# One hybrid encoder layer on one core: attention's unit issued as one group, the convolution's norm held back, and two weights prepared a head ahead

## The chip, the cores and the metric

The kernel runs on one core of one Trainium2 chip. The metric is the device time of one execution in microseconds (us), lower is better. The program is one launch, traced once in Python and ordered by a planner that works with simulated times.

## The reference

The layer works on 2048 tokens of 1024 channels (float32), with a memory of 256 rows for cross attention.

```python
y = rmsnorm(h, norm_mix_g) @ w_in                      # 3*512 for q, k, v; 2*512 for the convolution
att = dilated_sliding_attention(rotary(q), rotary(k), v)   # 8 heads of 64; windows (128,1), (512,4), (2048,16)
conv = silu(layernorm(depthwise_conv31(a * sigmoid(g)) + conv_b))
h = h + concat([att, conv]) @ w_out
xq, xk, xv = rmsnorm(h) @ w_xq, rmsnorm(mem) @ w_xk, rmsnorm(mem) @ w_xv     # 4 heads of 256
h = h + (softmax(xq @ xk.T / 16) @ xv) @ w_xo
h = h + square(relu(rmsnorm(h) @ w_up)) @ w_down       # 4096 hidden
return rmsnorm(h, norm_final_g)
```

The sliding attention computes three dilation patterns, each with its own softmax, and mixes them by their log-denominators. Every depthwise output sums 31 taps.

## The kernel before, in words

**Precision.** Almost every product is made of three: each operand is split into a high and a low float32r part, and `mm3` (lines 200 to 202) issues high x high and the two mixed products. A weight comes as `raw` by DMA, ScalarE copies its high part, VectorE subtracts to get the low part (lines 190 and 191; 385 and 386 in the memory stage).

**Stages.** First comes a memory stage (`memory`, together with `xprep`, which normalises and transposes x). It projects mem with w_xk (`pxk`), multiplies the result with the transposed w_xq, head by head, into `ascr` (`pa`), projects mem with w_xv (`pxv`) and multiplies that with w_xo into `bscr` (`pb`). So the passes need neither w_xq nor w_xo. Then follow the linear layers of w_in (`lin`, `lin_v` with its evictions `vst`, line 576), with the convolution's taps of token block 0 beside them (`cacc`, line 217, on VectorE). Then comes the far stage: attention of token block 0 (512 tokens) with all patterns, the far one among them, beside the rest of `lin` as filler and beside `conv_ln(0)`, the convolution's layer norm of block 0. Four passes follow, one for each block of 512 tokens: `post(p)` does w_out (`o`), the cross attention's scores (`xs`) and output (`x`), and the MLP (`up`, `dn`). Beside passes 0 to 2 run attention of the next block (`att(p + 1)`, 0.95 of its steps to a step of the pass) and the convolution of the next block (`conv`, 0.6 of a step). The last pass has no such side work.

**Attention's unit.** A unit is half of a head's block for one pattern. It has three pieces: scores `s` (four products of 256 columns, line 1003) with VectorE's mask and minimum (`sm`, line 774) and ScalarE's exponential (line 775); the turn, four transposes `pt` (line 781), copied into f16 `ph` by ScalarE and `pl` by VectorE (lines 784, 785); and `opt`, twelve f16 products with v (lines 789 to 791). A block has 32 near units (8 heads, 2 patterns, 2 halves). In `att`, a round steps the newest unit's scores, yields, then steps the turn of the unit before and `opt` of the one before that, and yields again. `combine` mixes the patterns (transposes `catT`, line 948).

**What sets the order.** Code is traced in the order that the generators are stepped (`weave`). Each engine executes its own queue in order. The planner fills the queues from simulated times: of the instructions that are ready on an engine it takes the one traced first, so a later one can go ahead while the earlier ones are not ready. `tc.issue_after(x)` forbids that for one engine: every instruction traced inside the block stays behind x on x's engine. `last` holds the last marked instruction of each engine, `after` opens such a block for some engines, and `pinned(gen, ...)` does so at each step of a generator. Marked on VectorE (`last["dve"]`) are, among others, the evictions in `lin`, `lin_v` and `post`, and attention's mask step.

**The norm.** `conv_ln(n)` loads the four channel groups (`lc`, from `cscr`), sums them (`lsum`, lines 240 to 242), takes column sums on TensorE (line 237), subtracts the mean (line 250), squares, divides, and applies silu. For block 0 it is pinned on TensorE alone; in the passes it is not pinned.

**The memory stage's tiles.** Its weights rotate through four sets of raw, high and low tiles (`wtiles`: two named with m..., two that borrow x's tiles). For w_xq a set is loaded, transposed on TensorE (`xqt`, line 416), copied (line 418) and subtracted (line 419).

Of the kernel before, what the change touches and what calls it, by code (L numbers as in the profile page):

```python
# [16 lines left out]
ALU = mybir.AluOpType  # L17
# [4 lines left out]
P = 128  # L22
S = 2048
D = 1024
# [6 lines left out]
XH = 4  # L31
# [12 lines left out]
def f(ap):  # L44
    return ap.bitcast(F32)


def hybrid_layer(ctx, tc, A, out):
# [7 lines left out]
    def dma(o, i, q=None):  # L56
        (q or nc.sync).dma_start(o, i)
# [10 lines left out]
    def ps(kind, name, shape=(P, 512), dtype=F32):  # L68

        if isinstance(banks[kind], str):  # L70
            kind = banks[kind]
        n = turn.get(kind, 0)
        turn[kind] = n + 1
        return psp.tile(list(shape), dtype, tag=f"bank{banks[kind][n % len(banks[kind])]}", name=name)
# [119 lines left out]
    def wcols(w, c0, n=P, rows=None):  # L194
        v = w.rearrange("(k p) m -> p k m", p=P)
        return v[:, :, c0:c0 + n] if rows is None else v[:, rows[0]:rows[1], c0:c0 + n]
# [151 lines left out]
    def memory(sp):  # L348
        nat = [load_nat(sp, A["mem"][0, P * j:P * (j + 1), :], f"mn{j}") for j in range(2)]
        mh, ml = ([xpool(q, i, 3, f"m{q}{i}", (P, 4, NMEM)) for i in range(2)] for q in "hl")  # L350
        for k2 in range(KC // 2):
            pt = ps("b", f"mt{k2}")
            for e in range(2):
                for j in range(2):
                    PE.transpose(pt[:, e * 256 + j * P:e * 256 + (j + 1) * P],
                                 nat_cols(nat[j], 2 * k2 + e), ident)
            for e in range(2):
                k = 2 * k2 + e
                hv, lv = mh[k // 4][:, k % 4, :], ml[k // 4][:, k % 4, :]
                src = pt[:, e * 256:(e + 1) * 256]  # L360
                ACT.activation(hv, src, AF.Copy, scale=gain("mem", k))
                DVE.scalar_tensor_tensor(lv, src, gain("mem", k), f(hv), op0=ALU.mult, op1=ALU.subtract)
        r = rstd_nat(sp, nat, "m")
        rb = ps("c", "rbm")
        bcast_rows(rb, r, 2)
        DVE.tensor_copy(rmem[:, 0:2], r[:, 0:2])
        rbm = sp.tile([P, 2, NMEM], F32, tag="rbm", name="rbm")
        for q in range(2):
            ACT.activation(rbm[:, q], rb[:, 0:NMEM], AF.Copy, scale=-1.0 / 16.0)
        yield  # L370
        cnt = [0]

        def wtiles(name, shape=(P, 8, P)):
            i = cnt[0] % 4
            cnt[0] += 1
            if i < 2:
                return [wp.tile(list(shape), dt, tag=t, name=f"m{t}_{name}", bufs=2)
                        for t, dt in (("raw", F32), ("whi", F32R), ("wlo", F32R))]
            return [xpool(q, j, 2, f"m{q}{j}_{name}", shape, dt)
                    for q, j, dt in (("h", i - 2, F32), ("h", i, F32R), ("l", i, F32R))]  # L380

        def split(src, name, shape=(P, 8, P)):
            raw, hi, lo = wtiles(name, shape)
            dma(raw, src)
            ACT.copy(hi, raw)
            DVE.tensor_tensor(lo, raw, f(hi), op=ALU.subtract)
            return hi, lo

        def proj(w, name, th, tl):

            for j in range(KC):
                wh, wl = split(wcols(w, j * P), f"{name}{j}")
                pt = ps("mm", f"p{name}{j}")[:, 0:256]
                for k in range(KC):
                    mm3(pt, wh[:, k, :], wl[:, k, :], mh[k // 4][:, k % 4, :], ml[k // 4][:, k % 4, :],
                        k == 0, k == KC - 1)
                hv, lv = th[j // 4][:, j % 4, :], tl[j // 4][:, j % 4, :]
                ACT.copy(hv, pt)
                DVE.tensor_tensor(lv, pt, f(hv), op=ALU.subtract)
                yield  # L400

        def ttiles(name):
            return [[xpool(q, 2 + i, 3, f"t{q}{name}{i}", (P, 4, NMEM)) for i in range(2)] for q in "hl"]

        th, tl = ttiles("k")
        yield from proj(w_xk, "xk", th, tl)
        for h in range(XH):
            wt = []
            for e in range(2):
                j = 2 * h + e  # L410
                raw, whi, wlo = wtiles(f"xq{j}")
                dma(raw, wcols(w_xq, j * P))
                for g in range(2):
                    pt = ps("b", f"xqt{j}{g}")
                    for i in range(4):
                        PE.transpose(pt[:, i * P:(i + 1) * P], raw[:, 4 * g + i, :], ident)
                    hv = whi[:, 4 * g:4 * g + 4, :].rearrange("p a b -> p (a b)")
                    ACT.copy(hv, pt)
                    DVE.tensor_tensor(wlo[:, 4 * g:4 * g + 4, :].rearrange("p a b -> p (a b)"), pt, f(hv),
                                      op=ALU.subtract)  # L420
                wt.append((whi, wlo))
                yield
            for k2 in range(4):
                pt = ps("mm", f"pa{h}{k2}")
                for q in range(2):
                    k = 2 * k2 + q
                    for e in range(2):
                        j = 2 * h + e
                        mm3(pt[:, q * 256:(q + 1) * 256], wt[e][0][:, k, :], wt[e][1][:, k, :],
                            th[j // 4][:, j % 4, :], tl[j // 4][:, j % 4, :], e == 0, e == 1)  # L430
                ev = t2(f"ea{h}{k2}")
                DVE.tensor_tensor(ev, pt, rbm.rearrange("p q m -> p (q m)"), op=ALU.mult)
                dma(ascr[h // 2, :, 2 * k2:2 * k2 + 2, 256 * (h % 2):256 * (h % 2) + 256],
                    ev.rearrange("p (q m) -> p q m", q=2))
            yield
        th, tl = ttiles("v")
        yield from proj(w_xv, "xv", th, tl)
        for h in range(XH):
            wt = []
            for e in range(2):  # L440
                wt.append(split(w_xo[(2 * h + e) * P:(2 * h + e + 1) * P, :], f"xo{2 * h + e}", (P, D)))
                yield
            for mc in range(2):
                for nh in range(2):
                    pt = ps("mm", f"pb{h}{mc}{nh}")
                    for e in range(2):
                        j = 2 * h + e
                        sl = slice(nh * 512, nh * 512 + 512)
                        ms = slice(mc * P, (mc + 1) * P)
                        mm3(pt, th[j // 4][:, j % 4, ms], tl[j // 4][:, j % 4, ms], wt[e][0][:, sl], wt[e][1][:, sl],  # L450
                            e == 0, e == 1)
                    ev = t2(f"eb{h}{mc}{nh}")
                    ACT.activation(ev, pt, AF.Copy, scale=rmem[:, mc:mc + 1])
                    dma(bscr[4 * nh:4 * nh + 4, :, 2 * h + mc, :].rearrange("m p c -> p m c"),
                        ev.rearrange("p (m c) -> p m c", c=P))
            yield

    def run(gens, steps):
# [222 lines left out]
    def ln_tiles(pl):  # L681
        def alloc(role, dtype, name, shape=(P, 512)):
            if role[:3] == "col":
                return pl.tile(list(shape), F32, tag="cl_" + role, name=name)
            if role[:2] == "cs":
                return pl.tile(list(shape), F32, tag="u" if role[2] < "2" else "acc", name=name, bufs=2)
            return pl.tile(list(shape), dtype, tag="vr", name=name, bufs=2)
        return alloc
# [13 lines left out]
    def conv(pl, n):  # L702

        yield from pinned(conv_units(pl, n), "dve")
        yield from conv_ln(n, ln_tiles(pl))

    def both(*gens):
        for _ in zip(*gens):
# [358 lines left out]
    def att(p, far=None):  # L1067


        comb = iter(())  # L1070

        def then(pr, o0):
            nonlocal comb
            drain(comb)
            comb = combine(p, pr, o0)
            next(comb)

        a = b = None
        for u in chain(att_units(p, far, then), (None, None)):
            if u:  # L1080
                next(u)
            yield
            if a:
                next(a)
            if b:
                next(b, None)
            next(comb, None)
            yield
            a, b = u, a
        for _ in comb:  # L1090
            yield
# [23 lines left out]
    with ExitStack() as st:  # L1115
# [19 lines left out]
                return aq.tile(list(shape), F32, tag={"cs2": "cth", "cs3": "ctl", "sum": "cat"}[role], name=name)  # L1135
            return t2(name, dtype)

        ln0 = pinned(conv_ln(0, ln_alloc), "pe")
        first = pinned(att(0, p2_), "pe")
        weave(islice(first, 50), (ln0, 0.33), (rest, 0.75))  # L1140
        drain(ln0)
# [460 lines left out]
```

## Time and profile before

| | |
|---|---|
| Median of 3 runs | 2862.2 us (2858.24 to 2862.79) |
| Profiled execution, its own time | 2865.75 us |
| Its span, first to last instruction | 2864.0 us |
| TensorE's mean granted clock in it | 0.993 |
| Busy: TensorE, VectorE, ScalarE, GpSimd | 2807.4, 1960.8, 1206.4, 467.7 us |
| Moved by DMA | 434.27 MB |

A row of the profile gives a line of the code, the engine, the operation and the tile written, then `<-` and the tiles read. PE is TensorE's matrix products, PEld its weight loads, DVE is VectorE, ACT is ScalarE, POOL is GpSimd, SP is the engine that issues DMAs. In the timeline the first two numbers are start and duration in us; what stands in brackets is the time that the engine was idle before, and what ended it. TensorE's products overlap, so the time that one takes from the others is the distance to the next start, which is shorter than its duration.

### The profile page before, as it was taken

Reading aid. Unit: us, or ns where it says so; the run is one execution under the profiler, and the core shown is the slowest. Engines: PE = TensorE matmul, PEld = TensorE weight load, DVE = VectorE, ACT = ScalarE, POOL = GpSimd, SP = SyncE. Lnnn points to the kernel's source line nnn. Section 1 sums busy time; section 2 is a strip of 40 time slices with the busy share of each in tenths; the row PEclk is TensorE's granted clock in tenths of the full one; section 3 lists DMA queues with packets and bytes.
Section 4 is the critical chain, followed back from the end, with each engine's and each line's share of the span. In section 5 each row is a group of like instructions: output and inputs, shape, how many; then the busy total and the mean of one; then the engine's idle time right before and its main releaser. Section 6 shows DMA issues by size and latency. Waiting matters only on the chain.

```text
span 2864.0 us, 41201 instructions
## 1 busy us (share of the span) xinstructions
PE 2807.4 (98%) x15440; PEld 2359.9 (82%) x15440; DVE 1960.8 (68%) x3473; ACT 1206.4 (42%) x2055; POOL 467.7 (16%) x483
## 2 busy tenths in 40 slices
PE   8999999999999999999999999999999999999998
PEld 7878899888788888888888888888888888888887
DVE  5736535455789777566887865579886646569886
ACT  5633211365544333434543344344433434444443
POOL 1337431131202011200021112001120110000000
PEclk9999999999999999999999999999999999999999
DMA  8979854699734544545444535534544455223332
GB/s 251 302 174 230 197 146 126 170 244 241 221 108 128 143 127 130 160 146 175 120 132 126 148 113 165 177 122 123 143 121 136 141 158 177 89 82 102 90 117 67
DMA packets 590730, 434.27 MB, mean 152 GB/s; under 512 B 191582, under 2 KB 508434, under 8 KB 590017
## 3 DMA queue, kind: packets, MB, share of 16 engines
q1 hardware_dynamic: 549776, 407.68, 50.5%
q10 hardware_dynamic: 38528, 17.93, 2.5%
q0 software_dynamic: 2224, 6.01, 0.6%
q8 instruction: 122, 2.00, 0.3%
q14 instruction: 80, 0.65, 0.1%
HBM read 340.42 MB, written 91.11 MB: 151 GB/s over the span
## 4 chain that ended last, share of the span: by engine, by line
PE 83%; DVE 8%; DMA 5%; issue 1%; ACT 1%; POOL 1%; SPq 1%; DVEq 0%; POOLq 0%; ACTq 0%
PE dn L200 8%; PE dn L201 8%; PE dn L202 8%; PE up L200 7%; PE up L202 7%; PE up L201 7%; PE lin L200 4%; PE lin L202 4%; PE lin L201 4%; PE o L200 2%; PE o L202 2%; PE o L201 2%; DVE cacc L217 2%; PE xs L200 2%; PE xs L202 2%; PE xs L201 2%
## 5 line engine op out<-in xcount | busy, mean ns | idle before, releaser
L200 PE MATMUL up<-mh,whi_u 128*128 128x512 f32 x1024 | 403.5, 394 | 0.4 <-ACT mh L1219 0.4
L201 PE MATMUL up<-ml,whi_u 128*128 128x512 f32 x1024 | 399.6, 390 | 2.1 <-DVE ml L1220 2.1
L202 PE MATMUL up<-mh,wlo_u 128*128 128x512 f32 x1024 | 399.1, 390 | 0.0
L217 DVE SCALAR_TENSOR_TENSOR cacc<-cu,cw,cacc 128x512 f32<-128x512 f32 x480 | 386.1, 804 | 5.4
L200 PE MATMUL dn<-hhh,whi_d 128*128 128x512 f32 x768 | 299.1, 399 | 1.1 <-ACT hhh L1331 1.1
L201 PE MATMUL dn<-hhl,whi_d 128*128 128x512 f32 x768 | 298.7, 391 | 0.7 <-DVE hhl L1332 0.7
L202 PE MATMUL dn<-hhh,wlo_d 128*128 128x512 f32 x768 | 298.2, 391 | 0.0
L190 ACT CAST whi_u<-raw_u 128x1024 fp32r<-128x1024 f32 x128 | 134.5, 1051 | 263.2 <-PE dn L201 188.7
L190 ACT CAST whi_d<-raw_d 128x1024 fp32r<-128x1024 f32 x100 | 105.1, 1051 | 319.9 <-PE up L201 281.5
L201 PEld LDWEIGHTS up<-ml,whi_u 128*128 128x128 f32 x1024 | 192.5, 188 | 40.9 <-DVE ml L1220 3.4
L202 PEld LDWEIGHTS up<-mh,wlo_u 128*128 128x128 f32 x1024 | 192.3, 188 | 40.4
L200 PEld LDWEIGHTS up<-mh,whi_u 128*128 128x128 f32 x1024 | 192.4, 188 | 38.0 <-ACT mh L1219 0.6
L191 DVE TENSOR_TENSOR wlo_u<-raw_u,whi_u 128x1024 fp32r<-128x1024 f32 x128 | 161.3, 1261 | 43.4 <-ACT whi_u L190 43.1
L1345 DVE TENSOR_TENSOR h<-h,dn 128x512 f32<-128x512 f32 x192 | 128.6, 683 | 84.7 <-PE dn L202 83.9
L1329 DVE SCALAR_TENSOR_TENSOR rl<-up,ssumx 128x512 f32<-128x512 f32 x96 | 66.0, 690 | 171.0 <-PE up L202 170.3
L774 DVE CUSTOM_DVE_ANT_0 sm<-s,mask 128x256 f32<-128x256 f32 (+1 forms) x384 | 128.6, 375 | 69.0 <-PE s L1003 45.2
L202 PEld LDWEIGHTS dn<-hhh,wlo_d 128*128 128x128 f32 x768 | 144.2, 188 | 30.7
L200 PEld LDWEIGHTS dn<-hhh,whi_d 128*128 128x128 f32 x768 | 143.7, 188 | 29.7 <-ACT hhh L1331 1.3
L201 PEld LDWEIGHTS dn<-hhl,whi_d 128*128 128x128 f32 x768 | 144.6, 188 | 28.3 <-DVE hhl L1332 1.5
L177 POOL TENSOR_TENSOR nr<-st_v,mhalf 128x4 f32<-128x4 f32 (+1 forms) x15 | 14.3, 951 | 817.2 <-DVE st_v L173 817.2
L775 ACT ACTIVATE sm<-sm,o 128x256 f32<-128x256 f32 (+1 forms) x288 | 116.5, 454 | 55.7 <-DVE o L774 55.3
L191 DVE TENSOR_TENSOR wlo_d<-raw_d,whi_d 128x1024 fp32r<-128x1024 f32 x100 | 128.2, 1282 | 14.2 <-ACT whi_d L190 14.1
(459 smaller groups left out, 7075.3 us busy)
## 6 DMA issues: line engine op xcount, KB each, us to landing
raw_u<-in_w_up_dram SPq DMA_DIRECT2D x128, 512.0 KB
raw_d<-in_w_down_dram SPq DMA_DIRECT2D x100, 512.0 KB
raw_o<-in_w_out_dram SPq DMA_DIRECT2D x32, 512.0 KB
raw_a<-ascr SPq DMA_DIRECT2D x32, 512.0 KB
raw_b<-bscr SPq DMA_DIRECT2D x32, 512.0 KB
b<-in_w_down_dram SPq DMA_DIRECT2D x28, 512.0 KB
k<-kscr SPq DMA_DIRECT2D x24, 512.0 KB
k<-kscr SPq DMA_DIRECT2D x8, 1152.0 KB
```

Source lines behind the costliest of these rows:

```text
L177: POOL.tensor_tensor(dst, v, mhalf.to_broadcast([P, v.shape[1]]), op=ALU.pow)
L190: ACT.copy(hi, raw)
L191: (lo_eng or DVE).tensor_tensor(lo, raw, f(hi), op=ALU.subtract)
L200: PE.matmul(o, lh, rh, start=first, stop=False, skip_group_check=more)
L201: PE.matmul(o, lh, rl, start=False, stop=False, skip_group_check=more)
L202: last["pe"] = PE.matmul(o, ll, rh, start=False, stop=end, skip_group_check=more)
L217: DVE.scalar_tensor_tensor(acc, u[:, t:t + 512], cw[:, c, t:t + 1], acc, op0=ALU.mult, op1=ALU.add)
L774: last["dve"] = DVE.tensor_tensor_reduce(dst, so, mask[:, 256 * m:256 * m + nk], 1.0, 3e38, ALU.add, ALU.min, mn)
L775: last["act"] = ACT.activation(dst, dst, AF.Exp, bias=mn, scale=-1.0)
L1329: last["dve"] = DVE.scalar_tensor_tensor(r, pt, 0.0, rsb, op0=ALU.max, op1=ALU.mult)
L1345: last["dve"] = DVE.tensor_tensor(hs[m], hs[m], pt, op=ALU.add)
```

## The change

There are three edits. In the memory stage, preparing a tile of w_xq (`turned_w`) and of w_xo (`rows_w`) becomes a function; heads 1 to 3 call it between the products of the head before, head 0 calls it where it was. The norm is pinned on VectorE too: for block 0 beside TensorE, in the passes alone. In `att` of blocks 1 to 3 (`far` is None) the scores of the newest unit move behind the turn and `opt` of the two units before, after the first yield; `opt` and the scores are each pinned behind the last marked TensorE instruction, which is the turn's last transpose and the last product of `opt`. The turn itself is not pinned. Attention of block 0 keeps its order.

```diff
+        def turned_w(j):
+
+            raw, whi, wlo = wtiles(f"xq{j}")
+            dma(raw, wcols(w_xq, j * P))
+            for g in range(2):
+                pt = ps("b", f"xqt{j}{g}")
+                for i in range(4):
+                    PE.transpose(pt[:, i * P:(i + 1) * P], raw[:, 4 * g + i, :], ident)
+                hv = whi[:, 4 * g:4 * g + 4, :].rearrange("p a b -> p (a b)")
+                ACT.copy(hv, pt)
+                DVE.tensor_tensor(wlo[:, 4 * g:4 * g + 4, :].rearrange("p a b -> p (a b)"), pt, f(hv),
+                                  op=ALU.subtract)
+            return whi, wlo
+
         th, tl = ttiles("k")
         yield from proj(w_xk, "xk", th, tl)
+        wts = [turned_w(0)]
+        yield
+        wts.append(turned_w(1))
+        yield
         for h in range(XH):
-            wt = []
-            for e in range(2):
...
-                wt.append((whi, wlo))
-                yield
+            wt, wts = wts, []
             for k2 in range(4):
                 pt = ps("mm", f"pa{h}{k2}")
...
                 dma(ascr[h // 2, :, 2 * k2:2 * k2 + 2, 256 * (h % 2):256 * (h % 2) + 256],
                     ev.rearrange("p (q m) -> p q m", q=2))
-            yield
+                if k2 % 2 == 0 and h < XH - 1:
+                    wts.append(turned_w(2 * h + 2 + k2 // 2))
+                    yield
+            yield
+
+        def rows_w(j):
+            return split(w_xo[j * P:(j + 1) * P, :], f"xo{j}", (P, D))
+
         th, tl = ttiles("v")
         yield from proj(w_xv, "xv", th, tl)
+        for j in range(2):
+            wts.append(rows_w(j))
+            yield
         for h in range(XH):
-            wt = []
-            for e in range(2):
-                wt.append(split(w_xo[(2 * h + e) * P:(2 * h + e + 1) * P, :], f"xo{2 * h + e}", (P, D)))
-                yield
+            wt, wts = wts, []
             for mc in range(2):
                 for nh in range(2):
...
+                if h < XH - 1:
+                    wts.append(rows_w(2 * h + 2 + mc))
+                    yield
             yield
...
         yield from pinned(conv_units(pl, n), "dve")
-        yield from conv_ln(n, ln_tiles(pl))
+        yield from pinned(conv_ln(n, ln_tiles(pl)), "dve")
...
         for u in chain(att_units(p, far, then), (None, None)):
-            if u:
+            if u and far:
                 next(u)
             yield
-            if a:
-                next(a)
-            if b:
-                next(b, None)
+            for g in (a, b, None if far else u):
+                with ExitStack() as st:
+                    if not far and g is not a:
+                        after(st, "pe")
+                    if g:
+                        next(g, None)
             next(comb, None)
             yield
             a, b = u, a
...
-        ln0 = pinned(conv_ln(0, ln_alloc), "pe")
+        ln0 = pinned(conv_ln(0, ln_alloc), "pe", "dve")
```

More of the change, by code (lines that the diff above doesn't have):

```diff
@@ L403, in ttiles @@
             return [[xpool(q, 2 + i, 3, f"t{q}{name}{i}", (P, 4, NMEM)) for i in range(2)] for q in "hl"]
+        def turned_w(j):
[10 more added lines that the diff above has]
+            return whi, wlo
         th, tl = ttiles("k")
         yield from proj(w_xk, "xk", th, tl)
+        wts = [turned_w(0)]
+        yield
+        wts.append(turned_w(1))
+        yield
         for h in range(XH):
-            wt = []
-            for e in range(2):
[L410 to L420, printed above, removed]
-                wt.append((whi, wlo))
-                yield
+            wt, wts = wts, []
             for k2 in range(4):
```

## The prediction

> **What bounds the kernel now.** I read the page first, for the busy shares and the chain that ended last.
>
> ```profile
> span 2864.0 us, 41201 instructions
> PE 2807.4 (98%) x15440; PEld 2359.9 (82%) x15440; DVE 1960.8 (68%) x3473; ACT 1206.4 (42%) x2055; POOL 467.7 (16%) x483
> PE 83%; DVE 8%; DMA 5%; issue 1%; ACT 1%; POOL 1%; SPq 1%; DVEq 0%; POOLq 0%; ACTq 0%
> ```
>
> TensorE is busy 98% of the span, and 83% of the chain that ended last is TensorE's. The change takes no matrix product away, so it can only win where TensorE stands still, runs slowly, or pays for going from one kind of product to another. What stands off TensorE in the chain, mostly DVE and DMA, tells where to look. The table of waits, for TensorE alone, names the places (total, times, longest):
>
> ```profile
> PE opt L791 <- DVE pl L785: 6.9, 9, 1.4
> PE lin L200 <- DVE vst L576: 4.1, 1, 4.1
> PE pa L200 <- ACT mwhi_xq L418: 3.2, 1, 3.2
> PE pa L202 <- DVE ml_xq L419: 2.2, 1, 2.2
> ```
>
> Three of these four bear on edits: lin on the held-back norm, the two pa on the prepared w_xq. I then went to each place with the timeline and with busy times by stretch.
>
> **The norm of block 0 (held behind VectorE's last marked instruction).** Here are the stretches around the 4.1 us wait (length; busy PE, PEld, DVE, ACT, POOL; TensorE's granted clock; DMA share; GB/s), then VectorE's timeline, the chain, and TensorE's timeline.
>
> ```profile
> 509.00:514.00 5.00, 0.91 (x5) 0.71 (x5) 4.86 (x9) 0.37 (x1) 0.00 (x0) 0.75 0.18 53
> 514.00:519.00 5.00, 5.00 (x14) 3.89 (x14) 1.58 (x4) 0.00 (x0) 0.00 (x0) 0.57 0.44 123
> ```
> ```profile
> 506.08 0.69 DVE L240 TENSOR_TENSOR lsum<-lc 128x512 f32<-128x512 f32 x1 [9.44 <-DMA lc<-cscr]
> 507.95 0.42 DVE L576 TENSOR_TENSOR vst<-v,vst 128x256 f16<-128x256 f32 x1
> ```
> ```profile
> 496.91 9.07 DMA lc<-cscr
> ```
> ```profile
> 513.56 0.80 PE L200 MATMUL lin<-xh,whi_g 128*128 128x512 f32 x1 [4.09 <-DVE vst L576]
> 514.15 0.63 PE L201 MATMUL lin<-xl,whi_g 128*128 128x512 f32 x1
> 518.62 0.39 PE L200 MATMUL lin<-xh,whi_g 128*128 128x512 f32 x1
> ```
>
> What is to be seen: lsum L240 is the first sum of conv_ln(0). Before the change only its TensorE instructions are pinned, so this VectorE sum was put early, ahead of the evictions of v (vst L576) and of the convolution's taps. Its data had not landed (the chain shows lc<-cscr in flight for 9.07 us), VectorE stood idle for 9.44 us, and everything behind it came late. TensorE had filled its PSUM banks and waited 4.09 us for a vst. That wait cost more than itself: the granted clock is 0.57 in the stretch after it. From 513.56 to 518.62 twelve products start in 5.06 us; twelve at the full-speed spacing of 0.23 us (seen further below, at 1345.62) take 2.8, so 2.3 us went to the slow clock.
>
> With the pin on "dve" the sums come behind the last marked VectorE instruction, and conv_ln(0) takes its first step only when attention's first units have been traced, which mark their own. So no sum can stand ahead of a vst. The load of lc is not moved and lands long before. Gain taken: 4.1 + 2.3 = 6.4 us. Behind it, the next thing that TensorE needs is the weight whi_g, which was there when it started at 513.56. The cost is that the norm's sums now stand among attention's VectorE work in the far stage:
>
> ```profile
> L241 DVE TENSOR_TENSOR lsum<-lsum,lc x4: 684/684/689, 507.3 to 2192.7; 128x512 f32<-128x512 f32 x4
> ```
>
> Three such sums are 3 x 0.684 = 2.1 us. I take 0, since they are short and TensorE has the filler products of lin beside them; +2.1 if each holds an eviction of attention up. In the passes the same pin keeps later sums from going ahead. No wait on them is among TensorE's, so I take 0 there.
>
> By the Trainium skill (TensorE: Matmul & The Clock Gate, Part 1) the clock halves after an idle window of about 3.4 us and needs about 3.4 us of work to recover. The trace agrees that a gap of this length halves it, and shows a longer recovery. An estimate from that page would put the slow clock at 1.7 us here, and the sum below 0.6 smaller.
>
> **The prepared w_xq and w_xo.** Stretches in the same columns, then ScalarE's and VectorE's timelines in two of them.
>
> ```profile
> 42.00:58.00 16.00, 12.59 (x86) 12.01 (x85) 9.51 (x15) 7.32 (x17) 3.84 (x3) 0.79 0.82 254
> 66.00:74.00 8.00, 7.12 (x57) 6.37 (x55) 5.91 (x15) 4.95 (x13) 2.31 (x2) 1.00 1.09 356
> 80.00:88.00 8.00, 5.51 (x46) 5.10 (x45) 8.00 (x11) 5.96 (x13) 4.57 (x2) 1.00 1.05 347
> 112.00:126.00 14.00, 13.10 (x73) 10.68 (x72) 7.99 (x11) 8.63 (x17) 1.29 (x1) 1.00 0.74 241
> ```
> ```profile
> 50.96 0.63 ACT L310 ACTIVATE junk<-xn 128x512 bf16<-128x512 f32 x1 [3.57 <-DMA xn<-in_x_dram]
> 51.59 0.56 ACT L418 CAST mwhi_xq<-xqt 128x512 fp32r<-128x512 f32 x1
> ```
> ```profile
> 82.12 3.43 DVE L386 TENSOR_TENSOR mwlo_xv<-mraw_xv,mwhi_xv 128x1024 fp32r<-128x1024 f32 x2
> 85.47 1.27 DVE L419 TENSOR_TENSOR ml_xq<-xqt,mh_xq 128x512 fp32r<-128x512 f32 x2
> ```
>
> The pattern is the same each time: a short copy or subtraction that TensorE needs (L418, L419) stands in its engine's queue behind something that waits or is long. The change moves, for heads 1 to 3, each tile's whole preparation (a load on SP's queue, eight transposes, two copies on ScalarE, two subtractions on VectorE) to between the products of the head before. The load passes two or three writes of ascr on SP's queue, the copies and subtractions pass as many evictions ea. The work is the same, only earlier, so each product has its operands ready up to one head sooner. In 66:74 TensorE stands 0.88 us and in 80:88 2.49 us; both fall in later heads, so I take 3.4 us. The first gap (3.41 us idle in 42:58, and a clock of 0.79, which costs 12.59 x 0.21 = 2.6) is head 0's. Head 0 is prepared where it was, behind the same junk that waits for x, so I take nothing there; 6.0 more if it goes too. For w_xo the idle time in 112:126 is 0.90 us, again behind a wait for x; I take half, 0.5. What hides the earlier preparation is TensorE's own work on the previous head. If the DMA engines are the limit (their share is 1.09 and 1.05 in the two stretches), the gaps only move, and the gain is 0; the earlier loads delay ascr and x then, and the bound below nothing is one more gap like that of 80:88, +2.5.
>
> **Attention's unit as one group.** TensorE's timeline shows what a change of kind costs (start, duration):
>
> ```profile
> 1345.28 0.19 PE L791 MATMUL opt<-v,pl 128*128 128x65 f16 x1
> 1345.30 0.48 PE L200 MATMUL xs<-whi_a,yh 128*128 128x512 f32 x1
> 1345.62 0.40 PE L201 MATMUL xs<-wlo_a,yh 128*128 128x512 f32 x1
> 1345.85 0.39 PE L202 MATMUL xs<-whi_a,yl 128*128 128x512 f32 x1
> ```
> ```profile
> 1034.13 0.19 PE L789 MATMUL opt<-v,ph 128*128 128x65 f16 x1
> 1034.15 0.47 PE L201 MATMUL dn<-hhl,whi_d 128*128 128x512 f32 x1
> 1035.63 0.20 PE L790 MATMUL opt<-v,ph 128*128 128x64 f16 x1
> 1035.97 0.36 PE L1003 MATMUL s<-k,qt 128*128 128x256 f32 x1
> 1036.17 0.29 PE L1003 MATMUL s<-k,ql 128*128 128x256 f32 x1
> 1036.29 0.28 PE L1003 MATMUL s<-k,qt 128*128 128x256 f32 x1
> ```
>
> The first xs after opt takes 0.32 us to the next start, the second 0.23; the first s after opt 0.20, the second 0.12. So each return from attention's transposes and f16 products to the others costs 0.08 to 0.09 us, whichever product comes next (0.087 in the median of the returns counted below). Putting s behind opt thus saves nothing by itself. What can be saved is returns in excess: at 1034.13 a unit's opt was cut after one product and resumed 1.5 us later, so it paid twice. In the pass between 1275 and 1820 us I counted 54 returns (from pt or opt to something else than a transpose), for 32 units; these are the first and the last.
>
> ```profile
> 1322.26 0.48 PE L200 MATMUL o<-cath,whi_o 128*128 128x512 f32 x1
> 1725.58 0.71 PE L200 MATMUL dn<-hhh,whi_d 128*128 128x512 f32 x2
> ```
>
> If every unit returned once, 22 x 0.087 x 3 passes = 5.7 us would go. The first piece of the group (pt) is not pinned, so the group can still be used as filler and be cut. A cut among the s products is free, and s is about 0.5 of the group's 0.44 + 0.36 + 0.5 us, so I take a third of it, 2.0 us. Bounds: -5.7, and +8.4 if each of 96 units is cut once more (96 x 0.087).
>
> The Trainium skill (TensorE: Matmul & The Clock Gate, Part 1, the queue depths) says that TensorE pulls weight loads ahead of matmuls in flight. If that held across kinds of product, a return would cost nothing and the group would gain 0; the rows above show that it costs. By that rule the sum would be 2.0 smaller.
>
> The added order is a wait of its own: opt of the second-last unit now stands behind pt of the last one, and the new s behind opt. And s is issued one half-step later, while pt stays where it was: two attention steps lie between them instead of three. A step is one main step of 24 products (24 x 0.23 = 5.5) over the rate 0.95, 5.8 us, so 11.6 instead of 17.4 us. What must fit in is short:
>
> ```profile
> L775 ACT ACTIVATE sm<-sm,o 128x256 f32<-128x256 f32 (+1 forms) x288 | 116.5, 454 | 55.7 <-DVE o L774 55.3
> ```
>
> Two of these and two of VectorE's mask steps come to under 2 us, so I take no cost, as long as the queues are not 9 us behind.
>
> **The sum.** 6.4 + 3.4 + 0.5 + 2.0 = 12.3 us. The profiled execution took 2865.75 us (span 2864.0), which becomes 2853.5. It was 3.5 above the median of the runs shown, 2862.2, which becomes 2849.9: **2850 us**. About 0.2%, 5.7 us, is what a measurement of this kernel can tell from no change.
>
> **The rivals.**
> *Only the norm pays (0.20).* The DMA engines limit the first 120 us, the gaps at pa move, and the units are cut as before. For it: DMA shares over 1. Against it: the gaps are behind ScalarE's and VectorE's queues, and later stretches have slack. 2862.2 - 6.4 = 2856.
> *The first gap goes too (0.08).* If the whole stage slips so that x has landed when junk is reached: 6.0 more, 2844.
> *The pin does nothing (0.07).* If the marked instruction at conv_ln(0)'s first step is an early one, the sum still goes ahead of vst. The 5.9 us of the other parts remain at best, and with the moving gaps nearly nothing: 2859. Against it: attention's first mask step is marked before.
> *Slower: attention's chain becomes late (0.13).* Where VectorE is full, the exponentials come too late for pt, pt stops TensorE's queue, and opt, s and the main products behind it stop with it. It decides where VectorE and ScalarE together run more than about 9 us behind. These stretches are the candidates:
>
> ```profile
> 850.00:930.00 80.00, 79.22 (x450) 65.10 (x449) 74.84 (x130) 38.86 (x66) 16.94 (x16) 1.00 0.43 122
> 1350.00:1460.00 110.00, 108.88 (x618) 90.00 (x617) 93.42 (x185) 52.99 (x103) 11.63 (x12) 1.00 0.38 112
> 1900.00:2030.00 130.00, 127.78 (x731) 105.10 (x730) 115.31 (x212) 62.42 (x118) 20.87 (x20) 1.00 0.41 116
> ```
>
> They are 320 us, 320/11.6 = 28 units. A wait like opt's on pl is 6.9/9 = 0.77 us: 28 x 0.77 = 21.5 us. Against the 12.3 gained that is +9: 2871. Against it: TensorE is idle only 0.8, 1.1 and 2.2 us in them now, and 9 us of slack are much.
>
> **How the numbers follow.** Forecast 0.52, rivals 0.20, 0.08, 0.07 and 0.13. The forecast alone spans about 2843 to 2857. The range leaves out the slower case and half of the pin's: 2838 (the forecast with the first gap and all 5.7 of the returns, 2850 - 6.0 - 3.7 = 2840, and a little for the spread of the runs) to 2863. Faster by over 0.2%: 0.50 of the forecast, 0.12 of the first rival and 0.08, together 0.70. Within: 0.02, 0.08 and 0.07, 0.17. Slower: 0.13.
>
> **What would show it.** Right: no wait of lin on vst L576 and no clock under 0.9 near 510 us; lsum L240 after 550 us; the waits of pa on ml_xq and ea gone; that on mwhi_xq near 48 us still there; some 45 returns in a pass instead of 54. Wrong: new waits of pt on sm, a new gap over 3 us with a slow clock behind it, or a far stage longer by what the first 550 us lost.

## The result, and the profile after

The changed kernel takes 2881.48 us in the median of six executions (2876.94 to 2882.85), beside 2858.14 us for the kernel before (2854.71 to 2862.79, six). The ratio is 1.0076, with a 95% interval of 1.0063 to 1.0089: slower by 0.76%, where I had forecast 2850 us and faster. The first two lines of the page of after:

```profile
span 2880.9 us, 41197 instructions
PE 2807.2 (97%) x15440; PEld 2361.5 (82%) x15440; DVE 1964.7 (68%) x3473; ACT 1212.7 (42%) x2055; POOL 462.8 (16%) x483
```

TensorE's busy time is the same as before (2807.4 us). By the page, all 16.9 us by which the span grew (2864.0 to 2880.9) are time in which TensorE stands still, so the table of its waits is the place to look. From the two timelines, the lengths between the first products of each stage, in us:

| stretch | before | after |
|---|---|---|
| start to first `lin` (memory stage) | 137.5 | 137.2 |
| first `v` to first `s` (the norm's place) | 146.6 | 140.1 |
| first `s` to pass 0 (far stage) | 195.4 | 190.9 |
| pass 0, pass 1, pass 2 | 552.5, 546.0, 544.1 | 563.7, 554.6, 552.5 |
| pass 3 to the end | 484.2 | 483.6 |

The three passes with attention beside them lose 28.2 us, and all the others together win some 11. Of the 28.2 us, 15.7 lie between the first `xs` and the first `up` of a pass. These are TensorE's waits in the passes (total, times, longest), first before:

```profile
PE up L201 <- DVE ml L1220: 2.1, 3, 0.9
PE catT L948 <- POOL cat L940: 1.5, 2, 1.2
PE opt L791 <- DVE pl L785: 1.4, 1, 1.4
```

and after:

```profile
PE catT L962 <- POOL cat L954: 6.4, 3, 3.0
PE x L200 <- ACT xp L1275: 4.2, 3, 1.4
PE ptx L1286 <- DVE ptl L1289: 2.9, 3, 1.0
PE xs L200 <- ACT xp L1275: 2.4, 3, 0.8
PE x L200 <- ACT pth L1288: 2.0, 3, 0.7
```

There are two groups in these rows. Four rows belong to the cross attention's softmax (`xp` is its exponential, `ptx` the turn of its probabilities), three times each, once in every pass. One row is `catT`, the transposes of attention's combined patterns, waiting for GpSimd. Neither is a wait inside the unit that the change grouped. The rows left out, of `dn`, `up`, `pt` and others, come to 12.4 us after and 6.8 before; no experiment here follows them one by one.

**The softmax, in three queues.** Before, around the step from `xs` to `x` in pass 0: TensorE, then VectorE, then ScalarE. The softmax works on four quarters; the first row is the last `xs` product of the first quarter.

```profile
839.75 0.39 PE L202 MATMUL xs<-whi_a,yl 128*128 128x512 f32 x1
844.86 0.39 PE L202 MATMUL xs<-whi_a,yl 128*128 128x512 f32 x1
845.09 0.28 PE L1003 MATMUL s<-k,qt 128*128 128x256 f32 x1
845.85 0.48 PE L200 MATMUL x<-pth,whi_b 128*128 128x512 f32 x1
```
```profile
841.04 0.68 DVE L1256 TENSOR_REDUCE xmx<-xs 128x2 f32<-128x512 f32 x1
842.29 0.22 DVE L1257 TENSOR_SCALAR xmx<-xmx,nr 128x2 f32<-128x2 f32 x1
```
```profile
842.61 0.56 ACT L1259 ACTIVATE xp<-xs,xmx,nr 128x256 f32<-128x256 f32 x1 [0.96 <-DVE xmx L1257]
846.10 1.04 ACT L190 CAST whi_b<-raw_b 128x1024 fp32r<-128x1024 f32 x1
```

The same place after:

```profile
830.16 0.40 PE L202 MATMUL xs<-whi_a,yl 128*128 128x512 f32 x1
834.28 0.39 PE L202 MATMUL xs<-whi_a,yl 128*128 128x512 f32 x1
834.51 0.60 PE L795 MATMUL pt<-ident,sm 128*128 128x128 f32 x4
835.75 0.28 PE L1017 MATMUL s<-k,ql 128*128 128x256 f32 x1
837.44 0.50 PE L200 MATMUL x<-pth,whi_b 128*128 128x512 f32 x1 [1.41 <-ACT xp L1275]
```
```profile
830.52 0.42 DVE L788 CUSTOM_DVE_ANT_0 sm<-s,mask 128x256 f32<-128x256 f32 x1
830.87 0.69 DVE L799 TENSOR_TENSOR pl<-pt,ph 128x512 f16<-128x512 f32 x1
832.47 1.28 DVE L1272 TENSOR_REDUCE xmx<-xs 128x2 f32<-128x512 f32 x2
834.93 0.35 DVE L1273 TENSOR_SCALAR xmx<-xmx,nr 128x2 f32<-128x2 f32 x2
```
```profile
834.75 1.05 ACT L190 CAST whi_b<-raw_b 128x1024 fp32r<-128x1024 f32 x1 [2.31 <-PE xs L202]
835.70 0.58 ACT L798 CAST ph<-pt 128x512 f16<-128x512 f32 x1
836.18 0.57 ACT L1275 ACTIVATE xp<-xs,xmx,nr 128x256 f32<-128x256 f32 x1
```

Before, the first exponential `xp` starts at 842.61, 2.5 us ahead of the first instruction behind the `xs` products (845.09). After, it starts at 836.18, 1.7 us behind it (834.51). On VectorE, the fresh unit's masks (`sm`), its neighbour's copy (`pl`) and taps of the convolution (`cacc`) now come in one bunch ahead of the steps of the softmax's minimum `xmx` and between them. On ScalarE, a weight's cast stands ahead of `xp` and waits 2.31 us for TensorE to finish `xs`. `x` reads `pth`, not `xp`, but `xp` reads the PSUM banks that `x` needs, so `x` waits until they are read.

At this place it isn't cover that is missing, that is, other work for TensorE while it waits for the next stage's input. From the end of the first quarter's `xs` (840.14 before, 830.56 after) TensorE has 5.7 us of other work until `x` before, and 5.5 us after, the unit's group from 834.51 to 836.03 among it. What grew is the softmax: from the same point to the end of the first quarter's second exponential it takes 3.6 us before (843.72) and 6.7 us after (837.29). When the first quarter's `xmx` is scaled, 2.2 of these 3.1 us are there on VectorE (842.51 and 835.15); the rest is ScalarE's cast and copy. In passes 1 and 2 all of these lengths are the same to 0.02 us.

At the next hand-over from engine to engine, the turn `ptx` and its copies, cover is missing too. TensorE before, then after:

```profile
855.19 0.63 PE L1270 MATMUL ptx<-ident,xp 128*128 128x128 f32 x4
855.58 0.37 PE L1003 MATMUL s<-k,qh 128*128 128x256 f32 x1
```
```profile
847.78 1.25 PE L1286 MATMUL ptx<-ident,xp 128*128 128x128 f32 x8 [0.96 <-DVE ptl L1289]
```

Before, a piece of a unit follows directly behind a stretch of `ptx` nine times in the three passes. After, it never does: the `ptx` stand together, and TensorE waits for their copies.

**catT.** VectorE, GpSimd and TensorE of after near 1210 us, then a window behind it (length; busy PE, PEld, DVE, ACT, POOL; granted clock; DMA share; GB/s):

```profile
1203.82 0.18 DVE L945 RECIPROCAL csm<-csm 128x8 f32<-128x8 f32 x1
```
```profile
1206.21 1.30 POOL L273 TENSOR_TENSOR ll<-lc,lh 128x512 fp32r<-128x512 f32 x1 [4.00 <-ACT lh L272]
1207.47 1.22 POOL L947 TENSOR_TENSOR ce<-ce,csm 128x24 f32<-128x24 f32 x1
1212.23 3.63 POOL L954 TENSOR_TENSOR cat<-cat,ld 128x512 f32<-128x512 f32 x2
```
```profile
1215.92 1.12 PE L962 MATMUL catT<-ident,cat 128*128 128x128 f32 x4 [3.03 <-POOL cat L954]
```
```profile
1215.00:1220.00 5.00, 4.08 (x12) 3.41 (x13) 3.29 (x4) 1.82 (x3) 0.86 (x1) 0.52 0.58 160
```

The combination's reciprocal `csm` is ready at 1204.0. Its next step `ce` stands on GpSimd behind `ll`, the last subtraction of the convolution's norm, for which GpSimd waits 4.00 us: `lh` on ScalarE, which `ll` needs, waits 3.71 us for the norm's own store. So `cat` is late, TensorE waits 3.03 us, and its clock is at 0.52 behind that. The pin in the passes, which holds the norm's VectorE steps back, is the suspect; `no_norm_pin` below tests it.

### The profile page after: what moved, and what is told of

It reads as the page before. It is cut to its first block, busy times and chain, and to the rows that moved or that the text cites. A ratio compares the mean times of both kernels' runs of the same rounds, so it can differ in the third digit from the quotient of the medians.

```text
span 2880.9 us, 41197 instructions
## 1 busy us (share of the span) xinstructions
PE 2807.2 (97%) x15440; PEld 2361.5 (82%) x15440; DVE 1964.7 (68%) x3473; ACT 1212.7 (42%) x2055; POOL 462.8 (16%) x483
## 5 line engine op out<-in xcount | busy, mean ns | idle before, releaser
L217 DVE SCALAR_TENSOR_TENSOR cacc<-cu,cw,cacc 128x512 f32<-128x512 f32 x480 | 394.3, 822 | 5.2
L836 POOL CAST qt<-qh 128x512 fp32r<-128x512 f32 x24 | 35.2, 1468 | 809.7 <-PE s L1017 763.9
```

The source lines that it names most:

```text
L217: DVE.scalar_tensor_tensor(acc, u[:, t:t + 512], cw[:, c, t:t + 1], acc, op0=ALU.mult, op1=ALU.add)
L836: POOL.tensor_copy(d.rearrange("p (b i) -> p b i", b=4), t.rearrange("p (i b) -> p b i", b=4))
```

## The experiments

All ratios are to the kernel before, run on the same chip in the same session; they stand in one table first, with the runs' medians in us. A ratio is taken over all runs of both kernels, so it differs a little from that of the medians.

| kernel | this | before | ratio, 95% interval |
|---|---|---|---|
| only_att | 2867.81 | 2853.78 | 1.0044, 1.0027 to 1.0061 |
| ln0_only | 2848.69 | 2853.78 | 0.9984, 0.9973 to 0.9995 |
| prep_only | 2855.97 | 2855.19 | 1.0005, 0.9995 to 1.0016 |
| old_att | 2849.49 | 2853.78 | 0.9986, 0.9976 to 0.9995 |
| no_norm_pin | 2868.15 | 2852.34 | 1.0052, 1.0033 to 1.0071 |
| no_pins | 2857.53 | 2853.78 | 1.0008, 0.9997 to 1.0019 |
| pin_s_only | 2872.43 | 2852.34 | 1.0068, 1.0050 to 1.0086 |
| pin_opt_only | 2860.17 | 2855.19 | 1.0014, 1.0005 to 1.0023 |
| comb_first | 2879.64 | 2852.34 | 1.0087, 1.0063 to 1.0111 |
| tied_mlp | 2856.54 | 2852.34 | 1.0011, 1.0001 to 1.0021 |
| tied_soft | 2866.98 | 2855.19 | 1.0037, 1.0025 to 1.0050 |
| tied_mlp_nn | 2848.60 | 2855.19 | 0.9974, 0.9964 to 0.9984 |

The theory to begin with was that the group in attention's loop costs all of the loss and more; its rivals put the loss on the norm's pin or on the preparation.

**Each edit by itself.** `old_att` is the whole change with attention's loop as before; `only_att` is the kernel before with the new loop alone; `ln0_only` has the pin on block 0's norm alone; `prep_only` has the weights' preparation alone.

```diff
 old_att
-            if u and far:
+            if u:
                 next(u)
             yield
-            for g in (a, b, None if far else u):
...
+            if a:
+                next(a)
+            if b:
+                next(b, None)
 only_att, against before: the same lines the other way round
 prep_only, against before: the change's lines in the memory stage
 ln0_only, against before
-        ln0 = pinned(conv_ln(0, ln_alloc), "pe")
+        ln0 = pinned(conv_ln(0, ln_alloc), "pe", "dve")
```

Expected of old_att: 

> The changed kernel with attention's loop as before (scores first, nothing pinned); the norm's pins and the early preparation stay. Theory G (the grouping costs about 28 us in the three passes, by gaps of TensorE at xs, x, ptx, catT and nrb, and the rest of the change gains about 11): 2847 us, no waits of x on xp or of ptx on ptl. Rival N (the norm's pin in the passes brings the gaps): 2875 us or more, the gaps stay. Rival M (the early preparation shifts the whole plan): likewise 2875 or more.

Expected of only_att: 

> The kernel before with attention's new loop alone. Theory G: 2858 + 28 = 2886 us, with the same gaps in each pass as in the changed kernel and the wait of lin on vst near 510 us still there. Rivals N and M: 2858, within 4 us.

Expected of ln0_only: 

> The kernel before with the pin of block 0's norm on VectorE alone. The prediction's term: 6.4 us less, 2852. If the far stage's further 4.5 us are this pin's too: 2847. If they belong to the attention loop or to the preparation: 2852.

Expected of prep_only: 

> The kernel before with the third edit alone: w_xq and w_xo prepared a head ahead. My prediction's term for it was -3.9 us, 0.9986. Rival D (the gaps only move, since each product of the stage is fed by transfers and by queues that the earlier preparation loads just as much): within 0.05% of 1; the start of w_xv's projection (near 90 us) and the first lin (near 137 us) then stand within 1 us of the kernel before.

Attention's loop alone costs 0.44%, less than the expected 2886 us. Its profile has the softmax's four rows with the numbers of the whole change and no wait of catT; its three passes are 12.6 us longer than those of before. Without the loop, the rest of the change is a gain of 0.14%. The pin on block 0's norm gives 0.16% (4.6 us of 2853.8), and the preparation nothing. The two edits that remain in old_att, the preparation and the pin in the passes, change nothing there (0.9986 beside 0.9984). But 0.44 - 0.16 + 0.05 is 0.33%, and the whole change measures 0.76%. So the pin in the passes, or another meeting of edits, has a price only where the unit is a group.

**The pin in the passes.** `no_norm_pin` is the whole change without it:

```diff
-        yield from pinned(conv_ln(n, ln_tiles(pl)), "dve")
+        yield from conv_ln(n, ln_tiles(pl))
```

Expected: 

> The whole change, but in the three passes the norm is not pinned on VectorE; for block 0 it is. Theory N (the pin in the passes pushes the norm's sums and GpSimd products into attention's combine, and TensorE waits for catT on top of the bunched group): attention alone cost +0.44% and the pin for block 0 gave -0.16%, so about 1.003 of the kernel before (2862 beside 2853.8), and the waits of catT on cat in the passes fall from 6.4 us to under 1.5. Rival P (the surplus comes from the earlier preparation, or from no part by itself but from the plan): stays at 1.0076 (2875), catT's waits may go or stay.

It measures 1.0052, 0.24% under the whole change, and the row of catT is gone from its waits. The two intervals overlap a little, so this step alone does not show the size. GpSimd at the same place:

```profile
1201.87 1.30 POOL L273 TENSOR_TENSOR ll<-lc,lh 128x512 fp32r<-128x512 f32 x1 [0.29 <-ACT lh L272]
1205.04 0.24 POOL L947 TENSOR_TENSOR ce<-ce,csm 128x24 f32<-128x24 f32 x1 [0.73 <-DVE csm L945]
1209.92 3.79 POOL L954 TENSOR_TENSOR cat<-cat,ld 128x512 f32<-128x512 f32 x2
```

The norm's last `ll` no longer waits in front of the combination. Counted from the start of pass 0, it begins at 474.9 us here and at 479.8 in the whole change, while `csm` is divided at nearly the same time (477.8 and 477.4). From the end of `csm` to the start of `cat`'s sum it is 5.0 us here (1204.95 to 1209.92) and 8.2 in the whole change. The 1.003 that I expected lies below the interval's lower end by a hair; whether the 0.2% between them is more than the spread stays open.

**Is the combination late by the new unit's masks?** `comb_first` steps it ahead of the new unit's scores:

```diff
-            for g in (a, b, None if far else u):
+            for n, g in enumerate((a, b, None if far else u)):
+                if n == 2:
+                    next(comb, None)
...
-            next(comb, None)
```

Expected: 

> The whole change, but the combination of the patterns is stepped ahead of the newest unit's scores, where it stood after them. Theory C (catT is late because the combination's VectorE work is queued behind the new unit's mask): catT's waits (6.4 us, and the slow clock behind the two that reach 3 us, about 3 us more) go, 1.0045 of the kernel before. Rival: catT is late by the norm on GpSimd; then its waits stay and the time is within 0.1% of 1.0076.

No: 1.0087, and catT still waits 6.1 us in all. (Of its three waits in the whole change only one reaches 3 us: 3.03, 2.41 and 0.93.) This theory falls, and GpSimd's queue remains.

**The pins of the group.** `no_pins` moves the scores but leaves out both TensorE pins; `pin_s_only` and `pin_opt_only` keep one.

```diff
 no_pins
-                    if not far and g is not a:
-                        after(st, "pe")
 pin_s_only
-                    if not far and g is not a:
+                    if not far and g is u:
 pin_opt_only
-                    if not far and g is not a:
+                    if not far and g is b:
```

Expected of no_pins: 

> The changed kernel with the scores still stepped behind the turn and opt, but without the two pins on TensorE. If the pins bring the gaps (the pieces of a unit can no longer fill different gaps): about 2848 us. If it is the move (the scores a half-step later, and combine's pins behind the new unit's mask and exponential): 2875 to 2882 us, with the waits of catT on cat and of x on xp as before.

Expected of pin_s_only: 

> The whole change, but of the two TensorE pins only that of the scores (behind opt's last product) is left; opt is not pinned behind the turn. If the scores' pin carries the loss (the new unit's mask and exponential start late and come bunched with the softmax): about 1.006 to 1.0076 of the kernel before. If opt's pin carries it (opt can no longer fill while the turn waits): about 1.001, as without both pins (1.0008). Shared: about 1.004.

Expected of pin_opt_only: 

> The whole change, but of the two TensorE pins only that of opt (behind the turn's last transpose) is left; the scores are free. The scores' pin alone measured 1.0068, none 1.0008, both 1.0076. If the costs add, about 1.0016 (2856.5). Rival (either pin alone closes the gap between the unit's pieces, so each costs nearly all): 1.005 or more.

Without both pins 1.0008 is left, 0.22% above old_att, which is the price of moving the scores; the pins make up the other three quarters (0.68%). Of these, the scores' pin carries nearly all: 1.0068 by itself, opt's 1.0014, both 1.0076. Yet pin_s_only doesn't lose where the whole change loses. Its waits in the passes are these:

```profile
PE up L200 <- ACT mh L1235: 5.1, 3, 1.7
PE dn L200 <- DVE h L1361: 4.9, 3, 2.0
PE up L201 <- DVE ml L1236: 2.5, 3, 1.4
```

The rows of `mh` and `ml`, the MLP's input, lie at a later hand-over, from `x` to `up`; that of `h`, the sum that empties the banks of `dn`, lies among the MLP's second products. Against old_att, the stretches from `xs` to `up` are only 1.0 us longer over the three passes, but those from `up` to `dn` 14.9 us. So it isn't the softmax as such. My reading is that TensorE used to have loose pieces of units to put in wherever it waits for VectorE and ScalarE between two stages of a pass. That the units' work on VectorE now comes in bunches fits these rows as well.

**Where in the pass.** `tied_mlp` makes a unit a group only beside the MLP, `tied_soft` only from the first `xs` to the last `x`; elsewhere the loop is the old one. `tied_mlp_nn` is tied_mlp without the norm's pin in the passes.

```diff
+            tied = tie[0] and not far
-            if u and far:
+            if u and not tied:
                 next(u)
             yield
-            for g in (a, b, None if far else u):
+            for g in (a, b, u if tied else None):
                 with ExitStack() as st:
-                    if not far and g is not a:
+                    if tied and g is not a:
...

 tied_mlp
+        tie[0] = True
         FG = 8
...
+        tie[0] = False                       # at the end of a pass
 tied_soft
+        tie[0] = True
         banks.update(xs=(0, 1, 2, 3), S=(4,))
...
+        tie[0] = False
         FG = 8
```

Expected of tied_mlp: 

> The whole change, but a unit is one group only beside the MLP (up and dn) of a pass; beside w_out and the cross attention (o, xs, x) it is stepped as before the change, without the two pins. Theory F (the loss is lost filler in the chain from xs to x: TensorE has nothing else to put into the gaps of the softmax): the waits of x and ptx on xp, pth and ptl fall from about 10 us to that of before, and the time to about 1.0045 of the kernel before (2866). Rival M (the loss sits beside the MLP): stays at 1.007 or more.

Expected of tied_soft: 

> The whole change, but a unit is one group only beside the cross attention, from the first xs to the last x; beside w_out and the MLP it is stepped as before the change. Theory S (the softmax between xs and x loses its place on VectorE and ScalarE to the unit's masks and copies): the stretches from xs to up lengthen by 5 to 6 us in each pass as in the full change, 15.7 us in all, so 0.9986 + 0.0055 = about 1.004 of the kernel before (2864 beside 2852). Rival (the loss is made by grouping over the whole pass, the attention arriving late at the softmax): under 1.001.

Expected of tied_mlp_nn: 

> The whole change, but a unit is one group only beside the MLP, and the norm is not pinned on VectorE in the passes. Theory N (the pin makes catT late where the group stands in front of it) with theory S: catT's 6.8 us of waits and the slow clock behind them go, 1.0011 - 0.0024 = about 0.9987. If the grouping also saved the returns that I predicted (2.0 us), 0.998. Rival (catT's waits come from the grouping alone): stays at 1.001.

tied_mlp measures 1.0011: without the group beside w_out and the cross attention, 0.65 of the 0.76% are gone, more than twice what I expected. Its largest wait is the other one of the two:

```profile
PE catT L963 <- POOL cat L955: 6.8, 3, 3.3
```

tied_mlp_nn takes that down to 2.6 us and measures 0.9974, 0.37% lower. So the two groups of waits come apart as the trace had them. In tied_soft, the softmax's four rows stand with the same numbers as in the whole change, and catT's is gone. The first two:

```profile
PE x L201 <- ACT xp L1277: 4.2, 3, 1.4
PE ptx L1288 <- DVE ptl L1291: 2.9, 3, 1.0
```

It measures 1.0037, beside old_att's 0.9986 half a per cent for this stretch, as expected. But the place is wider than I expected. In its profile, the stretches from `xs` to `up` are 10.4 us longer than old_att's over the three passes, not 15.7, and another 6.6 us are lost in pass 0 between `up` and `dn`:

```profile
908.00:915.00 7.00, 4.43 (x25) 3.34 (x25) 6.96 (x18) 5.93 (x13) 5.09 (x6) 0.91 0.54 119
915.00:921.00 6.00, 6.00 (x23) 4.80 (x22) 6.00 (x13) 3.16 (x7) 4.86 (x6) 0.82 0.27 77
```

VectorE is busy for 6.96 of 7 us there, and TensorE stands for 2.6 in short waits, 1.6 for VectorE and 1.0 for ScalarE. I take it that what the softmax has put off on VectorE comes due behind it; no run tests that by itself.

tied_mlp_nn is faster than both kernels, by 0.26% against before. That it also beats ln0_only (0.9974 beside 0.9984) isn't shown, since the intervals overlap.

## Why the prediction was wrong

**The norm of block 0: right place, a little too large.** TensorE's wait for vst is gone, and the clock with it is 1.00:

```profile
509.00:514.00 5.00, 5.00 (x27) 4.27 (x26) 0.42 (x1) 0.37 (x1) 0.00 (x0) 1.00 0.72 135
514.00:519.00 5.00, 5.00 (x23) 4.13 (x23) 0.00 (x0) 0.60 (x1) 1.84 (x2) 1.00 1.09 275
```

Against the profile of before this stretch is 6.5 us shorter (146.6 to 140.1), as I had summed it (6.4). Against the median it is 4.6 us (0.16%), because the wait isn't the same in each execution: two kernels that leave this edit out, only_att and prep_only, show it in their profiles with 1.1 and 2.8 us. Up to there only_att executes the same instructions in the same order on each engine as the kernel before; its `lc` came earlier, and VectorE waited 6.43 us for it instead of 9.44. I had taken a wait from one profile as if all executions had it. The sum lsum comes at 538.8 us, not behind 550 as I wrote, but behind the evictions all the same.

**The same pin in the passes: taken at 0, wrong in company.** With the old loop it costs nothing that the runs show, with the group 0.24% (no_norm_pin, barely clear of the spread) to 0.37% (tied_mlp_nn beside tied_mlp, clear of it). The sign that I had named, a new gap over 3 us with a slow clock behind it, came here: 3.03 us and 0.52. I had looked for waits on the sums on TensorE. I did not follow what the held-back norm does later on GpSimd, the queue it shares with the combination.

**The preparation: -3.9 predicted, 0 measured** (prep_only 1.0005, whose interval reaches from -1.4 to +4.6 us). Here is the end of w_xq in after, TensorE and VectorE:

```profile
84.37 0.39 PE L202 MATMUL pa<-thk,ml_xq 128*128 128x256 f32 x1 [2.60 <-DVE ml_xq L415]
```
```profile
80.29 3.42 DVE L386 TENSOR_TENSOR mwlo_xv<-mraw_xv,mwhi_xv 128x1024 fp32r<-128x1024 f32 x2
83.63 1.27 DVE L415 TENSOR_TENSOR ml_xq<-xqt,mh_xq 128x512 fp32r<-128x512 f32 x2
```

The last head's transposes come 2 us earlier, and the subtraction `ml_xq` stands behind the same two `mwlo_xv` of 3.42 us. The wait is 2.60 us, where it was 2.22. I had named that pair as the cause and then assumed that an earlier place in the code takes the subtraction past it. It didn't, and behind the longer wait the clock fell (0.83 over 80 to 88 us, 1.00 before). The wait on `ea` did go (0.7 us). For w_xo, TensorE's idle time in 112 to 126 is 0.87 us where it was 0.90. The stage is 0.3 us shorter in this profile, and its length varies from 133.9 to 137.7 us over all the kernels, with this edit or without.

**The group: -2.0 predicted, +12.6 measured alone (0.44% of 2853.8).** The counted returns fell from 54 to 49 in pass 1, not to 45, in pass 2 the same, and from 63 to 50 in pass 0. That is 23 x 0.087 = 2.0 us, so the saving itself was right in size, if not in where it came from. What failed is the sentence "the group can still be used as filler", and with it "I take no cost". I counted what the separate pieces cost TensorE and not what else they do: they fill TensorE while VectorE and ScalarE work on a stage's end, and they spread their own work on those engines. As one group they stand in one place instead of three, and their evictions fall on VectorE together. The price is in the waits of TensorE for the pass's own steps, 11.5 us in the softmax's four rows. The row to read for it was the stretch 850 to 930, where VectorE is busy 74.84 of 80 us; TensorE's idle time of 0.8 us in it did not show slack: VectorE had 5 us to spare in 80.

**The slower rival had the sign and one of the places.** I had priced it at 2871 us with 0.13, 9 us above the kernel before; measured are 23. Its mechanism, `pt` stopping TensorE for late exponentials, isn't what is seen: `pt` waits for `sm` only 1.1 us in the three passes of after. What stops are products of the pass itself, whose evictions come behind the unit's. It doesn't take 9 us of lag: the gap from `xs` to `x` opened by a softmax that was some 4 us later against TensorE.

**What stays open.** The experiments show which edits cost and where in the pass; they don't separate the lost cover from the bunches on VectorE, since the pins make both at once. Nor were VectorE's bunch and ScalarE's cast ahead of `xp` tried one by one; the trace shows 2.2 us of the one and 0.9 of the other. The three edits' own effects and the pin's 0.24% add up to 0.57%, and 0.76% is measured. The far stage is 4.5 us shorter in after, and varied from 188 to 195 us over the kernels with no edit that explains it.

## What to carry to other kernels

Before putting small pieces of side work together to save changes of kind, look at what lies next to them on TensorE: where they stand between the end of one stage and the start of the next, they can be the cover for that hand-over, and put together they also send their follow-up work to the other engines in one bunch, ahead of what that stage needs. Here this cost more than the changes of kind saved. A pin that is free by itself can cost where it meets another, because a held-back generator can arrive later on the other engines that it uses; follow it to its last step on the least busy one. A wait seen in one profile should be looked for in a second execution before its whole length goes into a sum.

## What the runs showed of the hardware

TensorE's clock fell behind shorter gaps than I had thought. In after, pass 1, and the stretches around it:

```profile
1771.92 1.11 PE L962 MATMUL catT<-ident,cat 128*128 128x128 f32 x4 [2.41 <-POOL cat L954]
```
```profile
1770.00:1772.00 2.00, 0.07 (x1) 0.08 (x2) 2.00 (x2) 1.04 (x1) 1.87 (x1) 0.88 0.00 0
1772.00:1774.00 2.00, 2.00 (x7) 1.81 (x8) 2.00 (x3) 0.94 (x2) 0.00 (x0) 0.50 0.48 92
```

A gap of 2.41 us is followed by a clock of 0.50, while the gap of 1.41 us ahead of `x` left it at 1.00. In tied_soft six waits of 0.26 to 1.02 us within 7 us, 3.0 us in all, did the same (0.50 at 914 to 916 us, part of the 0.82 over 915 to 921 above). The length alone doesn't decide it: in the memory stage, 2.10 us halved the clock in after (0.50 at 52 to 54), and 2.22 us in the kernel before left it at 1.00 (86 to 88). The Trainium skill (TensorE: Matmul & The Clock Gate, Part 1) gives the idle window as about 3.4 us and the sustained work until full speed as the same. The rows differ on the first: 2.41 us was enough. By the page's window the waits of catT would have cost their own length only; here the two longer ones (3.03 and 2.41 us) carried some products at half speed behind them. On the second, products ran at half speed for 3.0 us behind the gap of 2.41 us (1771.92 to 1774.97), near the page's figure, and for 6.0 us behind that of 3.03 us (1215.92 to 1221.95).
